# Turning tokens by products with diagonals, and a first gather that alternates with the gate product

## The chip, the core and the metric

The kernel runs on one core of a Trainium2 chip. TensorE (PE) multiplies, VectorE (DVE), ScalarE (ACT) and GpSimd (POOL) work elementwise, and SyncE (SP) issues the DMAs that bring weights from memory. The metric is the time of one execution in microseconds (us), as the median of several; one more execution was taken with a hardware profiler, and all rows below are from that one.

## The reference

A backbone of two layers over 256 latent tokens and, in the first layer, 256 context tokens, with 1024 features. Each layer has a token mixer of four branches and then a mixture of experts (MoE). The change touches the way into the MoE alone:

```python
h = rmsnorm(x, norm2_g) * (1.0 + mod[4]) + mod[3]     # per latent or context token
grp_prob = softmax(h @ w_grp + b_grp)                 # 4 groups, top 1
exp_logits = h @ w_exp + b_exp                        # 8 experts in the group, top 2
# every expert's tokens, gathered in blocks of rows:
hb = silu(xb @ w_gate[e]) * (xb @ w_up[e])
y = hb @ w_down[e]
x = x + mod[5] * (sum over a token's experts of weight * y)
```

There are 32 experts, and each has 6 MB of weights in float32.

## The kernel before

The stream of tokens is kept with features on partitions (`xT`: 128 partitions, 8 blocks of features, n tokens; n is 512 in layer 0 and 256 in layer 1). `moe(l)` does the following in each layer.

The squares of x have been summed in `acc`; `rstd_of` (L475 to L478) sums them over partitions by products with ones, and Ln and Exp on ACT make r, the inverse norm, the same on all partitions. In layer 0 the remaining modulation units (`self.later`, L440, L445, L452) are driven here. `route` scales the router's logits with r (L1267), brings them to tokens on partitions by products with a selection matrix (L1272), adds the bias (L1275) and runs a long chain of small steps on DVE, with a few products between (L1286 to L1417), which ends in `gm`, the masks by which tokens are gathered.

Beside this, the tokens are normed and modulated: L1539 multiplies x with r (blocks alternate between DVE and POOL), L1542 scales and shifts on ACT, L1547 turns 128 x 128 blocks by transposes on PE, and four lines split the turned block into a rounded part and the rest, `hk[0]` and `hk[1]` (L1553 on ACT, then either L1555 on DVE or L1558 on ACT and L1559 on POOL).

`gather` (L1424) multiplies `hk` with the masks, one group of products for each of the 8 blocks of features, and copies each to `xs` (L236 or L238). Two experts share a block of 128 rows. `group` then runs `up` for the gate weights and `up` for the up weights (L1440, 8 steps each), `turned`, `down` (L1482) and `add`.

Weights come in chunks of 1 MB into rings of buffers (`chunk`, L352): an expert has two for gate, two for up, two for down. There are 11 buffers in layer 0 and 15 in layer 1. SP issues the chunks in the program's order, and each issue waits until the buffer that it takes has been read for the last time. A gate product of two experts has two halves: the first reads the first chunk of each expert, the second half their second chunks.

The program's order on each engine is not that of the code: a scheduler places the instructions, so the pieces shown below come from the built programs.

Of the kernel before, what the change touches and what calls it, by code (L numbers as in the profile page):

```python
# [17 lines left out]
P = 128  # L18
D = 1024
# [166 lines left out]
class Net:  # L186
# [1067 lines left out]
            assert not self.main and not self.side and not any(self.left.values())  # L1254


    def route(self, l, n, r):

        nc = self.nc
# [4 lines left out]
        gi, ei, b64 = k[:, 0:4], k[:, 4:12], k[:, 45:53]  # L1264
        baser, capr, first = (self.slots[:, 256 + i * NE:256 + (i + 1) * NE] for i in range(3))
        lt = t([P, n], "lt")
        nc.vector.tensor_tensor(lt, self.lgp[:, 0:n], r, op=ALU.mult)  # L1267
        cum = t([P, nt + 1, NE], "cum", F32R)
        nc.gpsimd.memset(cum[:, 0].bitcast(F32), 0.0)
        p = self.ps("aux")  # L1270
        for i in range(nt):
            nc.tensor.matmul(p[:, i * 64:i * 64 + 36], lt[:, i * P:(i + 1) * P], self.k["sel"], start=True, stop=True)  # L1272
        lg = t([P, nt, 36], "lg")
        nv = n // NL
        nc.vector.tensor_tensor(lg.rearrange("p (v i) e -> p v i e", v=nv),  # L1275
                                p[:, 0:nt * 64].rearrange("p (v i e) -> p v i e", v=nv, e=64)[:, :, :, 0:36],
                                self.brow[:, :, None, :].to_broadcast([P, nv, nt // nv, 36]), op=ALU.add)
        sc = t([P, 8, nt], "sc")
        tt = nc.vector.tensor_tensor

# [123 lines left out]
    def gather(self, l, n, R, sid0, ns):  # L1404

        nc = self.nc
        nt = n // P
        ex = self.ex
        gm = ex.tile([P, nt, 4 * CAP], F32R, tag="gm", name=self.name("gm"), bufs=1)
        iota = self.slots[:, 0:ns]  # L1410
        sm = ex.tile([P, 2, nt], F32, tag="sm", name=self.name("sm"))
        for i in range(2):
            nc.vector.tensor_scalar(sm[:, i], R["s"][i], sid0, None, op0=ALU.subtract)
        for i in range(nt):
            tmp = ex.tile([P, 4 * CAP], F32, tag="gtmp", name=self.name("gtmp"), bufs=EXB[self.l][1])
            nc.vector.tensor_scalar(tmp[:, 0:ns], iota, sm[:, 0, i:i + 1], None, op0=ALU.is_equal)
            nc.vector.scalar_tensor_tensor(gm[:, i, 0:ns], iota, sm[:, 1, i:i + 1], tmp[:, 0:ns], op0=ALU.is_equal,  # L1417
                                           op1=ALU.add)
        xs = ex.tile([P, KD, 4 * CAP], F32, tag="xs", name=self.name("xs"), bufs=EXB[self.l][4])
        for k in range(KD):  # L1420
            p = self.ps("aux")
            for i in range(nt):
                for part, hh in enumerate(self.hk):
                    nc.tensor.matmul(p[:, 0:ns], hh[:, i, k * P:(k + 1) * P], gm[:, i, 0:ns],  # L1424
                                     start=i == 0 and part == 0, stop=i == nt - 1 and part == 1)
            self.copy(xs[:, k, 0:ns], p[:, 0:ns])
        return xs

    def up(self, ws, xs):
# [73 lines left out]
    def moe(self, l):  # L1503
        n = NT if l == 0 else NL
        nt = n // P
        nc, tc = self.nc, self.tc
        gate = self.mod[l][:, 40:48, :]
        a = self.a
        with ExitStack() as st:
            r1, r2 = self.ring1, self.pool(st, f"ring2{l}", RING2[l])  # L1510
            self.rings = [r for i in range(max(RING, RING2[l])) for r in [r1] * (i < RING) + [r2] * (i < RING2[l])]
            self.rt = self.pool(st, f"rt{l}", 1)
            self.slots = self.rt.tile([P, NSLOT], F32, tag="slots", name=f"slots{l}")
            nc.sync.dma_start(self.slots, a["consts"][:, slice(*CO[f"slots{l}"])])
            flat = lambda t: t.rearrange("p k t -> p (k t)")
            half = KD * NT // 2
            if l == 0:
                hk = [flat(self.big16(F32R, "hk")) for i in range(2)]
            else:
                b = flat(self.big16(F32R, "hk"))  # L1520
                hk = [b[:, 0:half], b[:, half:]]
                b = flat(self.big16(F32, "more"))
                more = [b[:, 0:half], b[:, half:], flat(self.xbig)[:, half:]]
                self.rings = [more] * len(more) + self.rings
            self.hk = [h.rearrange("p (i d) -> p i d", d=D) for h in hk]
            with ExitStack() as st2:
                h2p, mw = self.pool(st2, f"h2p{l}", 1), self.pool(st2, f"mw{l}", 4)
                self.work = mw
                r = self.rstd_of(self.acc[::-1], n, D)
                if self.later:  # L1530
                    rings, self.rings = self.rings, [r1]
                    self.drive(self.later)
                    self.rings, self.nchunk, self.later = rings, SHIFT, []
                R = self.route(l, n, r)
                h2 = h2p.tile([P, KD, n], F32, tag="h2", name=f"h2_{l}")
                A, B = self.A2[l], self.mod[l][:, 24:32, :]
                for k in range(KD):
# [5 lines left out]
                for i in range(nt):  # L1543
                    for q in range(2):
                        p = self.ps("mm")
                        for k in range(4):
                            nc.tensor.transpose(p[:, k * P:(k + 1) * P], h2[:, 4 * q + k, i * P:(i + 1) * P], self.ident)  # L1547

                        o = self.hk[0][:, i, q * 512:(q + 1) * 512]
                        lo = self.hk[1][:, i, q * 512:(q + 1) * 512]  # L1550
                        by4 = lambda t: t.rearrange("t (k f) -> t k f", k=4)
                        pv = p.rearrange("t (f k) -> t k f", k=4)
                        nc.scalar.copy(by4(o), pv)  # L1553
                        if q:
                            nc.vector.tensor_tensor(by4(lo), pv, by4(o).bitcast(F32), op=ALU.subtract)  # L1555
                        else:
                            h = self.w2()
                            nc.scalar.copy(by4(h), pv)  # L1558
# [12 lines left out]
            given = 2 * GROUPS[l].count("S")  # L1571
            for i, ranks in enumerate(groups):
                if i % 2 == 0:
                    xs = self.gather(l, n, R, float(i * P), min(2, len(groups) - i) * P)
                ws = [wsrc(r) if r < given else expert(R["tab"][0:1, r:r + 1]) for r in ranks]
                self.group(ws, xs[:, :, i % 2 * P:(i % 2 + 1) * P], R, float(i * P), gate, n, i + 1 == len(groups))
# [8 lines left out]
    def group(self, ws, xs, R, sid0, gate, n, last=False, now=False):  # L1585


        nc = self.nc
# [4 lines left out]
        p = self.up([w[0] for w in ws], xs)  # L1593
# [163 lines left out]
```

## Time and profile before

| | us |
|---|---|
| median of 3 runs | 2396.53 |
| lowest and highest | 2394.87, 2398.5 |
| the profiled execution | 2393.47 |
| its span in the trace | 2391.7 |
| PE busy (share of the span) | 2133.0 (89%) |
| DVE busy | 1240.1 (52%) |
| ACT busy | 767.8 (32%) |
| POOL busy | 471.0 (20%) |

The mean granted clock of PE was 0.967 of full speed. Busy time is an average over stages: in the mixers PE is busy nearly all the time, in the two MoE stages the DMA engines are. A float32 product shows as two records in the trace, so a count of records is twice that of instructions. PEld rows are loads of the stationary operand, PE rows the products; a row of the timeline may join several instructions of one line. What stands in brackets at a row's end is the idle time ahead of it and what ended it.

### The profile page before, as it was taken

The page shows a single profiled execution, that of the slowest core. Times are in us where ns is not written, and L with a number is a line of the kernel's source. Part 1 is how long each engine was busy: PE and PEld are TensorE (multiplying, and loading weights), DVE is VectorE, ACT ScalarE, POOL GpSimd, SP SyncE. Part 2 cuts the span into 40 slices and gives each one's busy share as a digit, 9 for nine tenths or more (in the row PEclk, how much of TensorE's full clock was granted, in tenths as well). Part 3 has the DMA queues.
Part 4 walks back from the last instruction along what each step waited for, and adds up shares of the span by engine and source line. Part 5 has one row for each costly group of instructions (what it writes and reads, how often), then busy time and mean ns, then how long its engine had stood idle before and what let it go on. Part 6 is the DMA issues. An engine that isn't in the chain of part 4 may idle for free. (4 is left out here: it accounts for less than half of the span.)

```text
span 2391.7 us, 30524 instructions
## 1 busy us (share of the span) xinstructions
PE 2133.0 (89%) x11634; PEld 1386.4 (58%) x11634; DVE 1240.1 (52%) x2344; ACT 767.8 (32%) x1394; POOL 471.0 (20%) x469
## 2 busy tenths in 40 slices
PE   6999999999999989989998978988989798877875
PEld 3878777867777753434432368887879642222311
DVE  4398887666434353434423268899777532111211
ACT  3434434356444231000100155555567310000001
POOL 2145443043311020000000033454352100000000
PEclk8999999999999989999999999999999899989998
DMA  8214423423354349999899933333235699999996
GB/s 310 88 56 139 141 100 112 170 77 124 116 183 156 126 197 414 421 407 421 350 421 421 379 124 106 107 110 103 71 108 175 258 382 421 421 421 421 421 421 262
DMA packets 174681, 577.75 MB, mean 242 GB/s; under 512 B 9152, under 2 KB 106048, under 8 KB 121024
## 3 DMA queue, kind: packets, MB, share of 16 engines
q1 hardware_dynamic: 172016, 571.27, 61.4%
q10 hardware_dynamic: 2512, 4.44, 0.5%
q8 instruction: 95, 1.56, 0.3%
q14 instruction: 58, 0.48, 0.1%
HBM read 573.58 MB, written 2.10 MB: 241 GB/s over the span
## 5 line engine op out<-in xcount | busy, mean ns | idle before, releaser
L527 PE MATMUL mm<-hhi,hi 128*128 128x512 f32 (+1 forms) x1216 | 441.4, 364 | 22.7 <-ACT hhi L506 6.8
L1440 PE MATMUL mm<-raw,xs 128*32 128x512 f32 (+2 forms) x1832 | 391.0, 624 | 66.1 <-DMA raw<-in_moe_w_up_dram 44.5
L529 PE MATMUL mm<-hlo,hi 128*128 128x512 f32 (+1 forms) x1216 | 425.0, 350 | 0.6 <-DVE hlo L507 0.6
L530 PE MATMUL mm<-hhi,lo 128*128 128x512 f32 (+1 forms) x1216 | 423.8, 349 | 0.7 <-DVE lo L374 0.7
L374 DVE TENSOR_TENSOR lo<-raw,hi 128x1024 fp32r<-128x1024 f32 x216 | 279.4, 1296 | 160.2 <-ACT hi L371 158.8
L371 ACT CAST hi<-raw 128x1024 fp32r<-128x1024 f32 x216 | 225.1, 1044 | 236.7 <-PE mm L529 163.5
L1440 PEld LDWEIGHTS mm<-raw,xs 128*32 128x32 f32 (+2 forms) x1832 | 106.0, 125 | 308.3 <-issue 178.0
L527 PEld LDWEIGHTS mm<-hhi,hi 128*128 128x128 f32 x1216 | 231.8, 191 | 70.1 <-ACT hhi L506 9.6
L1482 PE MATMUL mm<-raw,hT 128*32 128x512 f32 (+2 forms) x952 | 234.1, 598 | 23.7 <-DMA raw<-in_moe_w_down_dram 13.8
L530 PEld LDWEIGHTS mm<-hhi,lo 128*128 128x128 f32 x1216 | 231.1, 190 | 33.8 <-issue 1.2
L529 PEld LDWEIGHTS mm<-hlo,hi 128*128 128x128 f32 x1216 | 231.7, 191 | 31.6 <-DVE hlo L507 2.1
L1597 DVE TENSOR_TENSOR h<-h,mm 128x512 f32<-128x512 f32 x23 | 15.8, 687 | 369.7 <-PE mm L1440 369.7
L1055 POOL TENSOR_TENSOR acc<-acc,scr 128x512 f32<-128x512 f32 (+1 forms) x4 | 4.0, 995 | 970.8 <-ACT scr L1053 969.9
L882 DVE SCALAR_TENSOR_TENSOR w<-cvpad,vecs,w 128x512 f32<-128x512 f32 (+1 forms) x240 | 161.9, 674 | 3.9
L1482 PEld LDWEIGHTS mm<-raw,hT 128*32 128x32 f32 (+2 forms) x952 | 64.7, 122 | 158.2 <-issue 100.1
L1489 DVE SCALAR_TENSOR_TENSOR yl<-mm,sid,yh 128x512 fp32r<-128x512 f32 x46 | 34.4, 750 | 191.0 <-ACT yh L1488 189.0
L1488 ACT ACTIVATE yh<-mm,sid 128x512 fp32r<-128x512 f32 x46 | 31.6, 688 | 315.9 <-PE mm L1482 315.4
L1035 DVE SCALAR_TENSOR_TENSOR x<-aux,mod,x 128x256 f32<-128x256 f32 x288 | 116.5, 475 | 24.9 <-PE aux L1500 24.4
L1594 ACT ACTIVATE h<-mm 128x512 f32<-128x512 f32 x23 | 13.7, 597 | 277.4 <-PE mm L1440 277.4
L1424 PEld LDWEIGHTS aux<-gm,hk 128*128 128x128 f32 x608 | 79.0, 200 | 28.2 <-issue 20.0
L1424 PE MATMUL aux<-gm,hk 128*128 128x256 f32 (+1 forms) x608 | 86.5, 298 | 7.7 <-DVE gm L1417 7.7
L679 POOL TENSOR_TENSOR w<-w,w 128x256 f32<-128x256 f32 x96 | 89.4, 934 | 18.3 <-DVE w L680 17.8
(337 smaller groups left out, 3575.8 us busy)
## 6 DMA issues: line engine op xcount, KB each, us to landing
raw<-in_moe_w_up_dram SPq DMA_DIRECT2D x119, 1024.0 KB, 17.0
raw<-in_moe_w_down_dram SPq DMA_DIRECT2D x119, 1024.0 KB, 19.7
raw<-in_moe_w_gate_dram SPq DMA_DIRECT2D x110, 1024.0 KB, 19.1
raw<-in_w_in_dram SPq DMA_DIRECT2D x84, 1024.0 KB, 5.0
raw<-in_ada_w_dram SPq DMA_DIRECT2D x48, 1024.0 KB, 5.4
raw<-in_w_branch_dram SPq DMA_DIRECT2D x16, 1024.0 KB, 5.0
more<-in_moe_w_gate_dram SPq DMA_DIRECT2D x12, 1024.0 KB, 19.8
raw<-in_w_out_dram SPq DMA_DIRECT2D x8, 1024.0 KB, 5.0
```

Of the source, the lines that this page charges most:

```text
L371: self.nc.scalar.copy(hi, raw)
L374: eng.tensor_tensor(lo, raw, hi.bitcast(F32), op=ALU.subtract)
L527: nc.tensor.matmul(ps[j], wh, self.hhi[:, kk, 0:n], start=self.first(n, j, kk == 0), stop=False, skip_group_check=True)
L529: nc.tensor.matmul(ps[j], wh, self.hlo[:, kk, 0:n], start=False, stop=False, skip_group_check=True)
L530: nc.tensor.matmul(ps[j], wl, self.hhi[:, kk, 0:n], start=False, stop=kk == 7, skip_group_check=True)
L679: ptt(q4[:, :, B], q4[:, :, B], bc(p4[:, :, A, e:e + 1]), op=ALU.add)
L882: self.nc.vector.scalar_tensor_tensor(dst, s, w(i), dst, op0=ALU.mult, op1=ALU.add)
L1035: nc.vector.scalar_tensor_tensor(x, p[:, s], gate[:, dm, v:v + 1], x, op0=ALU.mult, op1=ALU.add)
L1424: nc.tensor.matmul(p[:, 0:ns], hh[:, i, k * P:(k + 1) * P], gm[:, i, 0:ns], start=i == 0 and part == 0, stop=i == nt - 1 and part == 1)
L1440: nc.tensor.matmul(p[s], xs[:, kk, s], r[:, k, :], start=kk == 0, stop=kk == 7, skip_group_check=True)
L1482: nc.tensor.matmul(p[s], hT[:, 2 * r + k, s], w[:, k, j * 512:(j + 1) * 512], start=r == 0 and k == 0, stop=r == 1 and k == 1, skip_group_ ...
L1489: nc.vector.scalar_tensor_tensor(yl, p, sid[:, 3:4], yh.bitcast(F32), op0=ALU.mult, op1=ALU.subtract)
```

## The change

The turning and the modulation become one product: a block of x (128 features by 128 tokens) is the stationary operand and a diagonal matrix with the modulation's scale (`dg`, 128 x 128) the moving one, so that the result has tokens on partitions. The shift is added by a product of one row with one row: the token's norm (`srow`) times the shift (`rows`). Four such products and one of one row fill a tile of 128 tokens by 512 features, and the eviction multiplies it by r, which is now a column with one number for each token (`rtok`): L1321 on ACT gives the rounded part, L1322 on DVE the rest. There are 8 such tiles in layer 0 and 4 in layer 1. `token_norm` makes `rtok` (L1264) and `srow` (L1271), `token_mod` the diagonals (L1290 on POOL for context tokens, in layer 0 alone; L1292 on ACT) and the shift's rows (8 products L1298). The router's logits are multiplied by r when their bias is added (L1342, once for each 128 tokens). In the first `gather` of a layer, each group of gather products is issued directly ahead of the step of the gate product that needs it.

```diff
+    def token_norm(self, l, n):
+        nt = n // P
+        p = self.ps("aux")
+        for i in range(nt):
+            for j, a in enumerate(self.acc[::-1]):
+                nc.tensor.matmul(p[:, i:i + 1], a[:, i * P:(i + 1) * P], self.ones[:, 0:1], start=i == 0 and j == 0,
+                                 stop=j == 1, skip_group_check=True)
+        r = self.norm.tile([P, 4], F32, tag="rtok", name=f"rtok{l}", bufs=1)[:, 0:nt]
+        nc.scalar.activation(r, p[:, 0:nt], AF.Ln, bias=self.eps, scale=1.0 / D)
+        nc.scalar.activation(r, r, AF.Exp, scale=-0.5)
+        p = self.ps("aux")
+        for j, a in enumerate(self.acc[::-1]):
+            nc.tensor.matmul(p[0:33, 0:n], self.ones[:, 0:33], a, start=j == 0, stop=j == 1)
...
+    def token_mod(self, l, n):
...
+        for v in range(n // NL):
+            nc.gpsimd.tensor_copy(bp[:, :, 32 * v], B[:, :, v])
+            d = self.work.tile([P, KD, P], F32, tag=f"dg{v}", name=f"dg{v}", bufs=1)
+            for k in range(KD):
+                if v:
+                    nc.gpsimd.tensor_scalar(d[:, k], self.ident, self.A2[l][:, k, v:v + 1], None, op0=ALU.mult)
+                else:
+                    nc.scalar.activation(d[:, k], self.ident, AF.Copy, scale=self.A2[l][:, k, v:v + 1])
...
+        for q in range(2):
+            p = self.ps("aux")
+            for k in range(4):
+                nc.tensor.matmul(p[0:33, k * P:(k + 1) * P], bp[:, 4 * q + k, :], self.ident, start=k == 0, stop=k == 3,
+                                 skip_group_check=True)
+            nc.scalar.copy(rows[:, q * 512:(q + 1) * 512], p[0:33])
...
+    def token_rows(self, l, n, r, s, by):
...
+                for k in range(4):
+                    o, x = p[:, k * P:(k + 1) * P], self.xT[:, 4 * q + k, i * P:(i + 1) * P]
+                    nc.tensor.matmul(o, x, by[0][v][:, 4 * q + k], start=k == 0, stop=False, skip_group_check=True)
+                e = slice(32 * v, 32 * v + 1)
+                nc.tensor.matmul(p, s[e, i * P:(i + 1) * P], by[1][e, q * 512:(q + 1) * 512], start=False, stop=True,
+                                 skip_group_check=True)
...
+                nc.scalar.activation(o, pv, AF.Copy, scale=r[:, i:i + 1])
+                nc.vector.scalar_tensor_tensor(lo, pv, r[:, i:i + 1], o.bitcast(F32), op0=ALU.mult, op1=ALU.subtract)
...
-        nc.vector.tensor_tensor(lt, self.lgp[:, 0:n], r, op=ALU.mult)
+        nc.vector.tensor_copy(lt, self.lgp[:, 0:n])
...
+        for i in range(nt):
+            nc.vector.scalar_tensor_tensor(lg[:, i], p[:, i * 64:i * 64 + 36], r[:, i:i + 1], self.brow[:, i * P // NL],
+                                           op0=ALU.mult, op1=ALU.add)
...
+        if first:
+            return xs, rows
+        for k in range(KD):
+            rows(k)
...
+                if rows:
+                    rows(kk)
...
-                h2p, mw = self.pool(st2, f"h2p{l}", 1), self.pool(st2, f"mw{l}", 4)
-                r = self.rstd_of(self.acc[::-1], n, D)
+                self.work = self.pool(st2, f"mw{l}", 2)
+                r, s = self.token_norm(l, n)
...
-                for k in range(KD):
-                    x, o = self.xT[:, k, 0:n], h2[:, k]
-                    (nc.gpsimd if k % 2 else nc.vector).tensor_tensor(o, x, r, op=ALU.mult)
-                    for v in range(n // NL):
-                        c = slice(v * NL, (v + 1) * NL)
-                        nc.scalar.activation(o[:, c], o[:, c], AF.Identity, bias=B[:, k, v:v + 1], scale=A[:, k, v:v + 1])
...
-                            nc.tensor.transpose(p[:, k * P:(k + 1) * P], h2[:, 4 * q + k, i * P:(i + 1) * P], self.ident)
...
-                            nc.gpsimd.tensor_tensor(lo, h, o.bitcast(F32), op=ALU.subtract)
+                self.token_rows(l, n, r, s, by)
```

PE in layer 0, from the norm to the router's small products (L475 the norm's sum, L440 and L452 the late modulation, L1272 the logits turned, L1547 the first transposes), before:

```order
L475 MATMUL aux_6374<-acc_6124,ones 128x512
L440 MATMUL mm_6388<-raw_6382,sT 32x512 x3
L440 MATMUL mm_6388<-raw_6384,sT 32x512 x4
L440 MATMUL mm_6388<-raw_6386,sT 32x512 x4
L452 MATMUL aux_6407<-cst,w_1051_6405 128x4 x4
L1272 MATMUL aux_6417<-cst,lt_6413 128x36 x4
L1547 MATMUL mm_6551<-cst,h_0_6526 128x128 x4
L1547 MATMUL mm_6560<-cst,h_0_6526 128x128
```

and after the change (L1264 and L1271 the norm, L1313 and L1315 the turning, L1298 the shift's rows, L1339 the logits turned):

```order
L1264 MATMUL aux_6371<-ones,acc_6124 128x1
L1271 MATMUL aux_6383<-acc_6124,ones 33x512
L440 MATMUL mm_6397<-raw_6391,sT 32x512 x3
L440 MATMUL mm_6397<-raw_6393,sT 32x512 x4
L440 MATMUL mm_6397<-raw_6395,sT 32x512 x4
L1313 MATMUL mm_6573<-dg_6425,x_6052 128x128 x4
L452 MATMUL aux_6416<-cst,w_1051_6414 128x4 x4
L1298 MATMUL aux_6445<-cst,bp 33x128 x4
L1298 MATMUL aux_6451<-cst,bp 33x128 x4
L1339 MATMUL aux_6461<-cst,lt_6457 128x36 x4
L1315 MATMUL mm_6573<-rows,srow 128x512
```

Seven of the eight L1264 stand just ahead of the second L1271, four products of the first tile have moved ahead of L452, and the eight L1298 stand between L452 and the logits.

DVE in layer 0, at the start of the selection chain (L1539 scales x, L1275 adds the bias, L1286 and the lines behind it are the selection), before:

```order
L1539 TENSOR_TENSOR h_0_6526<-x_6052,w_1045_6377 128x512
L1275 TENSOR_TENSOR lg_6422<-aux_6417,brow_6077 128x144
L1539 TENSOR_TENSOR h_0_6526<-x_6052,w_1045_6377 128x512
L1286 TENSOR_REDUCE sc_6424<-lg_6422 128x4
L1288 TENSOR_TENSOR goh_6426<-lg_6422,sc_6424 128x16
L1298 TENSOR_TENSOR ge_6432<-lg_6422,sc_6424 128x16
L1289 TENSOR_TENSOR goh_6426<-goh_6426,cst 128x16
L1291 TENSOR_REDUCE gohb_6429<-goh_6426 128x4
L1292 TENSOR_TENSOR goh_6426<-goh_6426,gohb_6429 128x16
L1300 TENSOR_REDUCE sc_6424<-ge_6432 128x4
L1303 TENSOR_TENSOR e_0_6437<-lg_6422,goh_6426 128x128
```

and after (L1342 scales and adds the bias, L1352 to L1369 are the same selection steps, L1322 takes the rest of a turned tile):

```order
L1342 SCALAR_TENSOR_TENSOR lg_6466<-aux_6461,rtok_6380,brow_6077 128x36 x4
L1352 TENSOR_REDUCE sc_6471<-lg_6466 128x4
L1354 TENSOR_TENSOR goh_6473<-lg_6466,sc_6471 128x16
L1364 TENSOR_TENSOR ge_6479<-lg_6466,sc_6471 128x16
L1355 TENSOR_TENSOR goh_6473<-goh_6473,cst 128x16
L1357 TENSOR_REDUCE gohb_6476<-goh_6473 128x4
L1322 SCALAR_TENSOR_TENSOR hk_6367<-mm_6573,rtok_6380,hk_6366 128x512
L1358 TENSOR_TENSOR goh_6473<-goh_6473,gohb_6476 128x16
L1366 TENSOR_REDUCE sc_6471<-ge_6479 128x4
L1369 TENSOR_TENSOR e_0_6484<-lg_6466,goh_6473 128x128
L1367 RECIPROCAL sc_6471<-sc_6471 128x4
```

The products with r are gone from DVE, and the first of eight L1322 stands between two steps of the selection; the others follow at similar distances.

PE in layer 1, at the first gather (L1424 or L1491 the gather products, L1440 or L1514 the gate product), before:

```order
L1424 MATMUL aux_15545<-gm_15504,hk_15327 128x256 x4
L1424 MATMUL aux_15551<-gm_15504,hk_15327 128x256 x4
L1424 MATMUL aux_15557<-gm_15504,hk_15327 128x256 x4
L1440 MATMUL mm_15564<-raw_15565,xs_15514 64x512
L1440 MATMUL mm_15564<-raw_15567,xs_15514 64x512
```

and after:

```order
L1491 MATMUL aux_15555<-gm_15538,hk_15348 128x256 x4
L1491 MATMUL aux_15563<-gm_15538,hk_15348 128x256 x3
L1514 MATMUL mm_15550<-raw_15551,xs_15548 64x512
L1514 MATMUL mm_15550<-raw_15553,xs_15548 64x512
L1491 MATMUL aux_15563<-gm_15538,hk_15348 128x256
L1491 MATMUL aux_15571<-gm_15538,hk_15348 128x256 x4
L1514 MATMUL mm_15550<-raw_15551,xs_15548 64x512
L1514 MATMUL mm_15550<-raw_15553,xs_15548 64x512
L1514 MATMUL mm_15550<-raw_15551,xs_15548 64x512
L1514 MATMUL mm_15550<-raw_15553,xs_15548 64x512
```

The gate product no longer waits for the last gather group: its first step has two groups of the gather ahead of it, and the rest alternates.

## Rows read from the trace of the kernel before

**Rows 1.** The page, moved GB/s in 40 equal slices of the span.

```profile
GB/s 310 88 56 139 141 100 112 170 77 124 116 183 156 126 197 414 421 407 421 350 421 421 379 124 106 107 110 103 71 108 175 258 382 421 421 421 421 421 421 262
```

**Rows 2.** 20-us windows inside the plateaus: busy time by engine, PEclk, DMA share, GB/s.

```profile
920.00:940.00 20.00, 16.69 (x109) 5.97 (x102) 10.60 (x29) 0.60 (x1) 0.00 (x0) 0.97 1.02 422
...
2020.00:2040.00 20.00, 11.55 (x68) 2.50 (x64) 0.00 (x0) 0.60 (x1) 0.00 (x0) 0.95 1.01 421
```

**Rows 3.** Windows of 1 us at the edges of the two holes.

```profile
884.00:885.00 1.00, 1.00 (x6) 1.00 (x6) 0.84 (x6) 0.00 (x0) 0.00 (x0) 0.50 0.19 74
897.00:898.00 1.00, 1.00 (x8) 0.41 (x6) 0.00 (x0) 0.00 (x0) 0.00 (x0) 1.00 0.39 57
1919.00:1920.00 1.00, 1.00 (x10) 0.87 (x10) 0.51 (x2) 0.42 (x2) 0.00 (x0) 1.00 0.58 238
1924.00:1925.00 1.00, 1.00 (x6) 0.29 (x4) 0.00 (x0) 0.00 (x0) 0.00 (x0) 1.00 0.62 82
```

**Rows 4.** Timeline, SP's DMA issues: start, duration, line, tile, count.

```profile
860.70 35.95 SPq L352 DMA_DIRECT2D raw<-in_moe_w_down_dram  x4
...
1923.49 0.33 SPq L352 DMA_DIRECT2D raw<-in_moe_w_gate_dram  x1
```

**Rows 5.** Timeline, layer 0 from the norm to the gate product.

```profile
854.60 1.13 PE L475 MATMUL aux<-acc,ones 128*128 128x512 f32 x2
...
859.69 1.05 PE L452 MATMUL aux<-cst,w 128*128 128x4 f32 x8 [1.25 <-ACT w L445]
...
864.03 0.16 DVE L1286 TENSOR_REDUCE sc<-lg 128x4 f32<-128x16 f32 x1
...
877.32 1.36 DVE L1366 TENSOR_TENSOR tmp<-O,slot 128x128 f32<-128x128 f32 x1
...
882.25 2.11 PE L1424 MATMUL aux<-gm,hk 128*128 128x256 f32 x7 [4.20 <-DVE gm L1417]
...
892.64 13.95 PE L1440 MATMUL mm<-raw,xs 128*64 128x512 f32 x64
```

**Rows 6.** Prices: timeline rows, groups of the page's part 5, a window of L1424 alone.

```profile
907.97 1.95 PE L1398 MATMUL aux<-cst,s 128*128 128x128 f32 x16
...
L1489 DVE SCALAR_TENSOR_TENSOR yl<-mm,sid,yh 128x512 fp32r<-128x512 f32 x46 | 34.4, 750 | 191.0 <-ACT yh L1488 189.0
L1488 ACT ACTIVATE yh<-mm,sid 128x512 fp32r<-128x512 f32 x46 | 31.6, 688 | 315.9 <-PE mm L1482 315.4
...
891.80 0.42 DVE L236 COPY xs<-aux 128x256 f32<-128x256 f32 x1 [1.47 <-PE aux L1424]
...
888.00:892.00 4.00, 4.00 (x36) 4.00 (x35) 1.00 0.00 0
```

**Rows 7.** Timeline, layer 1 from the norm to the gate product.

```profile
1894.54 0.70 PE L475 MATMUL aux<-acc,ones 128*128 128x256 f32 x2 [0.26 <-DVE acc L1055]
...
1898.94 0.15 DVE L1286 TENSOR_REDUCE sc<-lg 128x2 f32<-128x8 f32 x1
...
1904.07 1.26 DVE L1325 TENSOR_TENSOR cum<-cum,Os 128x32 fp32r<-128x32 f32 x1
...
1913.56 2.75 PE L1424 MATMUL aux<-gm,hk 128*128 128x256 f32 x11 [3.49 <-DVE gm L1417]
...
1919.81 12.67 PE L1440 MATMUL mm<-raw,xs 128*64 128x512 f32 x58
```

**Rows 8.** 5-us windows with the granted clock (PEclk, after the busy times).

```profile
860.00:865.00 5.00, 2.02 (x18) 1.80 (x17) 4.87 (x12) 2.59 (x7) 3.56 (x3) 0.89 1.01 423
865.00:870.00 5.00, 3.12 (x10) 1.92 (x10) 4.64 (x30) 4.85 (x11) 0.70 (x2) 0.50 1.01 426
880.00:885.00 5.00, 2.75 (x11) 2.58 (x12) 4.84 (x22) 0.00 (x0) 0.02 (x1) 0.59 0.84 349
1910.00:1915.00 5.00, 1.51 (x7) 1.44 (x7) 4.64 (x30) 0.18 (x1) 0.00 (x0) 0.50 1.01 419
1915.00:1920.00 5.00, 5.00 (x30) 4.87 (x30) 1.63 (x5) 1.20 (x4) 0.00 (x0) 0.64 0.94 385
```

More of the change, by code (lines that the diff above doesn't have):

```diff
@@ L1254, in mixer @@
             assert not self.main and not self.side and not any(self.left.values())
+    def token_norm(self, l, n):
+        nc = self.nc
+        nt = n // P
[10 more added lines that the diff above has]
+            nc.tensor.matmul(p[0:33, 0:n], self.ones[:, 0:33], a, start=j == 0, stop=j == 1)
+        s = self.work.tile([33, n], F32, tag="srow", name="srow", bufs=1)
+        nc.scalar.activation(s, p[0:33, 0:n], AF.Ln, bias=self.eps[0:33], scale=1.0 / D)
+        nc.scalar.activation(s, s, AF.Exp, scale=0.5)
+        return r, s
@@ new lines, in token_mod @@
+    def token_mod(self, l, n):
+        nc = self.nc
+        B = self.mod[l][:, 24:32, :]
+        bp = self.work.tile([P, KD, 33], F32, tag="bp", name="bp", bufs=1)
+        nc.gpsimd.memset(bp, 0.0)
+        dg = []
+        for v in range(n // NL):
[6 more added lines that the diff above has]
+                    nc.scalar.activation(d[:, k], self.ident, AF.Copy, scale=self.A2[l][:, k, v:v + 1])
+            dg.append(d)
+        rows = self.work.tile([33, D], F32, tag="rows", name="rows", bufs=1)
+        for q in range(2):
[4 more added lines that the diff above has]
+            nc.scalar.copy(rows[:, q * 512:(q + 1) * 512], p[0:33])
+        return dg, rows
@@ new lines, in token_rows @@
+    def token_rows(self, l, n, r, s, by):
+        nc = self.nc
+        by4 = lambda t: t.rearrange("t (k f) -> t k f", k=4)
+        for q in range(2):
+            for i in range(n // P):
+                v = i * P // NL
+                p = self.ps("mm")
+                for k in range(4):
[4 more added lines that the diff above has]
+                                 skip_group_check=True)
+                o = by4(self.hk[0][:, i, q * 512:(q + 1) * 512])
+                lo = by4(self.hk[1][:, i, q * 512:(q + 1) * 512])
+                pv = p.rearrange("t (f k) -> t k f", k=4)
+                nc.scalar.activation(o, pv, AF.Copy, scale=r[:, i:i + 1])
+                nc.vector.scalar_tensor_tensor(lo, pv, r[:, i:i + 1], o.bitcast(F32), op0=ALU.mult, op1=ALU.subtract)
@@ L1273, in route @@
         lg = t([P, nt, 36], "lg")
[L1274 to L1277, printed above, removed]
+        for i in range(nt):
+            nc.vector.scalar_tensor_tensor(lg[:, i], p[:, i * 64:i * 64 + 36], r[:, i:i + 1], self.brow[:, i * P // NL],
+                                           op0=ALU.mult, op1=ALU.add)
         sc = t([P, 8, nt], "sc")
@@ L1402, in spread, with gather @@
                 nc.scalar.copy(R[src, i], p[:, 0:n])
-    def gather(self, l, n, R, sid0, ns):
+    def gather(self, l, n, R, sid0, ns, first=False):
         nc = self.nc
@@ L1419, in gather, with rows @@
         xs = ex.tile([P, KD, 4 * CAP], F32, tag="xs", name=self.name("xs"), bufs=EXB[self.l][4])
-        for k in range(KD):
+        def rows(k):
             p = self.ps("aux")
@@ L1426, in gather, with up @@
             self.copy(xs[:, k, 0:ns], p[:, 0:ns])
+        if first:
+            return xs, rows
+        for k in range(KD):
+            rows(k)
         return xs
-    def up(self, ws, xs):
+    def up(self, ws, xs, rows=None):
         nc = self.nc
@@ L1526, in moe @@
             with ExitStack() as st2:
-                h2p, mw = self.pool(st2, f"h2p{l}", 1), self.pool(st2, f"mw{l}", 4)
-                self.work = mw
-                r = self.rstd_of(self.acc[::-1], n, D)
+                self.work = self.pool(st2, f"mw{l}", 2)
+                r, s = self.token_norm(l, n)
                 if self.later:
@@ L1533, in moe @@
                     self.rings, self.nchunk, self.later = rings, SHIFT, []
+                by = self.token_mod(l, n)
                 R = self.route(l, n, r)
-                h2 = h2p.tile([P, KD, n], F32, tag="h2", name=f"h2_{l}")
-                A, B = self.A2[l], self.mod[l][:, 24:32, :]
-                for k in range(KD):
-                    x, o = self.xT[:, k, 0:n], h2[:, k]
-                    (nc.gpsimd if k % 2 else nc.vector).tensor_tensor(o, x, r, op=ALU.mult)
-                    for v in range(n // NL):
-                        c = slice(v * NL, (v + 1) * NL)
-                        nc.scalar.activation(o[:, c], o[:, c], AF.Identity, bias=B[:, k, v:v + 1], scale=A[:, k, v:v + 1])
[L1543 to L1546, printed above, removed]
-                            nc.tensor.transpose(p[:, k * P:(k + 1) * P], h2[:, 4 * q + k, i * P:(i + 1) * P], self.ident)
[L1549 to L1558, printed above, removed]
-                            nc.gpsimd.tensor_tensor(lo, h, o.bitcast(F32), op=ALU.subtract)
+                self.token_rows(l, n, r, s, by)
             self.ex = self.pool(st, f"ex{l}", 2)
@@ L1572, in moe @@
             for i, ranks in enumerate(groups):
-                if i % 2 == 0:
+                rows = None
+                if i == 0:
+                    xs, rows = self.gather(l, n, R, 0.0, 2 * P, True)
+                elif i % 2 == 0:
                     xs = self.gather(l, n, R, float(i * P), min(2, len(groups) - i) * P)
                 ws = [wsrc(r) if r < given else expert(R["tab"][0:1, r:r + 1]) for r in ranks]
-                self.group(ws, xs[:, :, i % 2 * P:(i % 2 + 1) * P], R, float(i * P), gate, n, i + 1 == len(groups))
+                self.group(ws, xs[:, :, i % 2 * P:(i % 2 + 1) * P], R, float(i * P), gate, n, i + 1 == len(groups), rows=rows)
             if l + 1 < DEPTH:
@@ L1583, in moe, with group @@
             self.rings = [self.ring1]
-    def group(self, ws, xs, R, sid0, gate, n, last=False, now=False):
+    def group(self, ws, xs, R, sid0, gate, n, last=False, now=False, rows=None):
         nc = self.nc
@@ L1592, in group @@
         o = h.rearrange("s (r k f) -> s r k f", r=2, k=2)
-        p = self.up([w[0] for w in ws], xs)
+        p = self.up([w[0] for w in ws], xs, rows)
         nc.scalar.activation(o, src(p), AF.Silu)
```

## The prediction

> **What bounds the kernel.** I read the page's forty slices first. In the GB/s row [rows 1] two plateaus of 421 GB/s stand out: one from slice 16 to 23, the experts of layer 0, one from slice 33 to the end, the experts of layer 1. Inside them the DMA engines are full and PE is not: 16.69 of 20 us busy with a DMA share of 1.02 in layer 0, 11.55 of 20 with 1.01 in layer 1 [rows 2]. So in both plateaus the end is set by when the stream of weight chunks starts and by nothing that PE, DVE or ACT do later. A chunk is 1 MB, at 421 GB/s 2.5 us.
>
> The stream does not start cleanly. Before each plateau the ring of weight buffers is full and nobody frees one. The one-microsecond windows show the edges: in layer 0 the DMA share falls to 0.19 at 884 us and comes back only at 897 (a hole of 13 us); in layer 1 it falls at 1919 and comes back at 1924, a hole of 4.9 us from 1919.6 to 1924.4 by those windows' shares [rows 3]. SP, which issues all chunks in order, shows the same thing: a stretch that starts at 860.70 lasts 35.95 us since its last DMA has to wait for a buffer, and in layer 1 the next issue comes at 1923.49 [rows 4]. What frees the buffer is the first gate product (L1440), and that starts at the end of the gather: 892.64 in layer 0 [rows 5], 1919.81 in layer 1 [rows 7]. A whole gate product is 32 records of 0.215 us (6.9 us). Its first half frees two chunks, 3.4 us after its start (896.1 and 1923.25, where SP's issues follow), its second half two more. Hence the only thing that the change can move for the whole kernel is the pair of moments "first two chunks free" and "gate product done", once in each layer. The most that layer 1 can gain is its hole, 4.9 us; layer 0 has 13.
>
> **Layer 0, up to the selection.** Between the second L475 at 854.60 and the router's small products PE now has seven products L1264 more (a weight load each, so the price of L452, 1.05 us for 8 records, two records an instruction: 0.26) = 1.8 us; L1271 costs what the L475 that it replaces did. The four L1313 that the order puts in front of L452 take 4 x 0.244 (L1398: 16 records, 8 instructions, 1.95 us [rows 6]) = 1.0 us and lie in the 1.25 us that PE waits there for ACT [rows 5]. Eight L1298 add 8 x 0.244 = 1.95, on the path. L1339 then starts near 864.3 and no longer waits for r on 512 columns, but four scaled additions (0.2 each) follow where one stood. The first reduction of the selection, 864.03 before, comes near 866.0: +2.0 us.
>
> **Layer 0, the selection.** From that reduction to the gather the trace has 882.25 - 864.03 = 18.2 us. About 4.7 us of it is work of the old turning in the way: L1555 subtractions on DVE (some 1.6 visible), DVE operations stretched while POOL's L1559 ran (L1366 took 1.36 us, where its like take 0.3, and one L1348 likewise: 2.0), ACT and PE steps queued behind evictions and transposes (1.1). POOL's part and the transposes go. In their place eight L1322 of 0.75 (by L1489, which has the same form) stand in DVE's order; two fall in waits that DVE has anyway, six are visible: 4.5 us, and 0.5 for the interleaved products. Net +0.3. The gather starts near 884.5, and its last mask (1.65 us later) is there at 886.2.
>
> **Layer 0, first gather with the gate product between.** After the last mask, at full clock: 59 gather products of 0.118 (36 records, two of them in part, fill 4 us [rows 6]; 7.0), eight steps of the gate product of 0.86 (6.9), and 1.2 for steps that wait for the copy of xs (0.42 each [rows 6], mostly beside the next gather group) = 15.1. The product is done at 901.3 (before 899.5), but its first half already at 893.9 (before 896.1), since only half of the gather stands ahead of it. So two chunks flow 2.2 us earlier, and then the stream pauses: the third needs the whole product, 901.3 + 1.1 (SP's issue to first data, as before) = 902.4. Before, the third followed the first two without a pause at 902.2. Sum for layer 0: **+0.2 us**. If the products run at the lower clock for long, +2 instead.
>
> **Layer 1.** Here token_mod has half the diagonals and no late modulation is waited for: 0.73 + 0.5 + 1.95 us from 1894.54 bring L1339 to 1897.7 and the first reduction to 1898.8 (before 1898.94). The chain to the gather was 1913.56 - 1898.94 = 14.6 us [rows 7]. What goes is a hold by L1539 (0.7), DVE stretched beside POOL (L1325 took 1.26 where 0.2 is its like, and L1346 likewise: 2.0) and one visible L1555 (0.5): 3.2. What comes is two visible L1322, 1.5. The gather starts near 1911.75 (-1.8). Up to the first two free chunks there are 20 gather products and 4 steps: 2.4 + 3.4 = 5.8 at full clock. The granted clock was 0.50 when the old gather began and came back inside it [rows 8]; with the same 4.7 us of half clock as before, 2.4 more, and 0.5 of waits: 1920.45, first data 1921.5 (before 1924.4). The whole product is done at 1925.8, the third chunk follows at 1926.9 where it was 1929.4. Sum for layer 1: **-2.4 us**.
>
> Together -2.2: 2393.47 becomes 2391.3 for the profiled execution. The median of the runs shown is 3.06 above the profiled one, so **2394.3**.
>
> **Costs that the trace of before does not show.** The one-row products L1315 (128x512 from one partition): between the 0.244 of L1313 and the 1.13 that an L475 took with its tail [rows 5]; I take 0.9, near the second, since the moving columns are the same (at 0.244 the tiles of layer 0 would end 5 us earlier, with the chain then held by L1322 alone, no more than 0.5 us off the sum). L1321 (eviction with a scale) and L1322: L1488 and L1489 at 0.69 and 0.75, against 0.6 and 0.67 of what they replace. The 16 diagonals (8 on ACT, 8 on POOL, layer 0) lie beside L440 and the norm; were they late, up to 2.5 us. Bounds for layer 0: -2.5 (no L1322 visible) to +8 (rival C); for layer 1: -4.9 (its hole) to +1.5 (all L1322 visible and no gain from POOL).
>
> **Rival B: the clock stays up.** The rows show the granted clock at 0.89 from 860, 0.50 from 865 and 0.59 from 880, and 0.50 at 1910 [rows 8], each time after several microseconds in which PE had only small products between waits. In the changed kernel PE is busy without a gap from 855 to 880 and from 1894 to 1905. If the level of 2.4 GHz holds through the gathers, layer 1's first chunks are free 2.9 us before the forecast, inside the old plateau, and the hole of 4.9 us is gone; layer 0 gains about 1 (0.8 on the products inside the selection). -5.9: **2390.6**. Against it: between the last turning product and the gather there are still some 5 us of selection, as there were before the old falls. The Trainium skill ("TensorE: Matmul & The Clock Gate", Part 1) calls the reduced clock the default that activity lifts; the rows agree as far as the fall after sparse work goes, and no row here has such a dense stretch just ahead of a gather.
>
> **Rival C: slower.** DVE's order is fixed, and the first L1322 stands before the selection's sixth step. Each L1322 waits for a tile of PE (four L1313 and one L1315) and for ACT's L1321. At full clock a tile is 1.9 us and the chain is hardly held. At 0.50, the level that the trace has over just these microseconds [rows 8], a tile is 2 x (0.96 + 0.86) = 3.6, eight tiles from 864.7 end at 893.8, and the selection's steps, the rank products behind the tiles on PE too, follow their pace: gather at about 892 instead of 884.5, +7.5 in layer 0; in layer 1 four tiles end at 1912.3, the gather at 1913.5, +1 after the lost gain. **2405**. It decides once the tiles take over 2.5 us each.
>
> **Rival D: the alternation costs.** If each of the eight steps waits for its own copy with nothing between (0.6 us each, 4.8 a layer), the product ends 3.6 later in each layer: layer 0 +3.8, layer 1 +1.2: **2401**. Against it: the order has a gather group or two ahead of each step.
>
> **How the numbers follow.** Forecast 0.53, B 0.21, C 0.15, D 0.11. Two runs of this kernel differ by up to 0.15%, so 0.2% (4.8 us) is the least that counts: faster is below 2391.7, slower above 2401.3. The forecast's own range is 2391 to 2398. Faster: B's larger part (0.19) and the low end of the forecast (0.08) = 0.27. Slower: C (0.15) and a third of D (0.04), less a little of C that lands short = 0.17. The rest, 0.56, is within. For 8 in 10 the range takes in B down to 2388.5 and D up to 2401.5.
>
> **What would show it.** Right: the holes' ends in the DMA windows at about 895 and 1921.5 with a second, short hole near 901 in layer 0; the first L1440 step right after the first gather group; gather starts near 884.5 and 1911.75; L1322 at 0.75 without long waits ahead. A granted clock of 1.0 at 1912 speaks for B, a clock of 0.5 at 866 and idle DVE ahead of L1322 for C, PE waits of 0.5 us before each step of the gate product for D. I am wrong if the plateaus do not move with the first release, or if the mixers' stretch before 854 changes, where nothing was touched.

## The result, and the profile after

The changed kernel takes 2415.9 us (median of 4, 2410.47 to 2417.37) against 2395.8 for the kernel before: a ratio of 1.0081, 95% interval 1.0067 to 1.0096. It is slower by 20 us, where I forecast 2 us less. The profiled execution has a span of 2415.6 us, 23.9 more than the one before.

The timeline shows where. These are SP's rows of the changed kernel; L1588 loads the slot table and marks the start of a MoE stage, the second column is the length of a row:

```profile
858.26 0.43 SPq L1588 DMA_DIRECT2D slots<-in_consts_dram  x1
...
864.28 50.20 SPq L352 DMA_DIRECT2D raw<-in_moe_w_down_dram  x4
915.29 23.44 SPq L352 DMA_DIRECT2D raw<-in_moe_w_gate_dram  x8
...
1914.28 0.33 SPq L1588 DMA_DIRECT2D slots<-in_consts_dram  x1
...
1945.97 0.33 SPq L352 DMA_DIRECT2D raw<-in_moe_w_gate_dram  x1
```

SP's long wait in layer 0 is 50.20 us where it was 35.95 [rows 4]. I measure each stage from its own slot table, since the mixers ahead of it, in which the change moved no instruction, differ from one execution to the next: in the eleven profiled executions of this study the first table is loaded between 854.8 and 859.0. From that mark, layer 0's gather starts at 43.71 (before 27.15) and layer 1's at 22.15 (before 20.79). The 23.9 us are, from SP's rows: 3.2 ahead of layer 0; 19.9 from its table to the second set of up chunks (80.71 against 60.79), 16.6 of them before the gather starts; -1.6 from there to layer 1's table; and 2.4 from that table to the end (501.32 against 498.93).

The DVE rows of the selection, with one of ACT between, say what the gather waited for. In brackets stand the idle time ahead of a row and what ended it:

```profile
876.46 0.75 DVE L1322 SCALAR_TENSOR_TENSOR hk<-mm,rtok,hk 128x512 fp32r<-128x512 f32 x1 [2.19 <-ACT hk L1321]
...
879.74 0.69 ACT L1321 ACTIVATE hk<-mm,rtok 128x512 fp32r<-128x512 f32 x1 [2.13 <-PE mm L1315]
...
899.71 0.75 DVE L1322 SCALAR_TENSOR_TENSOR hk<-mm,rtok,hk 128x512 fp32r<-128x512 f32 x1 [3.00 <-ACT hk L1321]
```

Seven of the eight L1322 wait for ACT, 12.7 us in all (two are shown), and ACT's L1321 waits for PE. PE's rows in the same stretch, one tile after another:

```profile
867.85 1.12 PE L1315 MATMUL mm<-rows,srow 1*128 1x512 f32 x2
868.90 1.16 PE L1313 MATMUL mm<-dg,x 128*128 128x128 f32 x8
869.99 1.70 PE L1315 MATMUL mm<-rows,srow 1*128 1x512 f32 x2
871.62 2.08 PE L1313 MATMUL mm<-dg,x 128*128 128x128 f32 x8
873.63 2.07 PE L1315 MATMUL mm<-rows,srow 1*128 1x512 f32 x2
875.63 2.08 PE L1313 MATMUL mm<-dg,x 128*128 128x128 f32 x8
...
896.88 2.07 PE L1315 MATMUL mm<-rows,srow 1*128 1x512 f32 x2
...
901.97 3.15 PE L1491 MATMUL aux<-gm,hk 128*128 128x256 f32 x12 [3.02 <-DVE gm L1483]
```

The same two lines take 1.1 us each at first and 2.1 from 871 on: a tile goes from 2 us to 4. The last ends at 898.95, and the gather follows 3.0 us later. The windows give the reason (busy time of PE, PEld, DVE, ACT and POOL, then the granted clock, the DMA share and GB/s):

```profile
865.00:870.00 5.00, 5.00 (x36) 3.88 (x35) 1.91 (x11) 1.95 (x4) 0.00 (x0) 1.00 1.01 423
870.00:875.00 5.00, 5.00 (x13) 2.56 (x12) 3.39 (x15) 0.69 (x1) 0.29 (x1) 0.54 1.02 421
875.00:880.00 5.00, 5.00 (x12) 2.65 (x12) 1.88 (x10) 1.15 (x3) 0.29 (x1) 0.50 1.01 421
885.00:890.00 5.00, 5.00 (x15) 2.98 (x13) 2.20 (x12) 0.95 (x2) 0.00 (x0) 0.50 0.48 200
...
900.00:905.00 5.00, 3.03 (x12) 2.71 (x12) 4.81 (x23) 0.00 (x0) 0.00 (x0) 0.50 0.00 0
905.00:910.00 5.00, 4.93 (x19) 2.26 (x19) 0.15 (x3) 0.37 (x1) 0.00 (x0) 0.71 0.00 0
```

PE is busy in all of 865 to 890, and yet the granted clock falls from 1.00 to 0.50 (of the levels 2.4 and 1.2 GHz, the lower) and stays there to 907, when the gate product has begun. Before, the clock fell too [rows 8], but PE then had only short pieces of work; here it has no gap.

### The profile page after: what moved, and what is told of

Same layout as the page of the kernel before. It is cut to its first block, busy times and chain, and to the rows that moved or that the text cites. A ratio compares the mean times of both kernels' runs of the same rounds, so it can differ in the third digit from the quotient of the medians.

```text
span 2415.6 us, 30778 instructions
## 1 busy us (share of the span) xinstructions
PE 2178.0 (90%) x11762; PEld 1412.5 (58%) x11762; DVE 1235.8 (51%) x2346; ACT 762.8 (32%) x1388; POOL 458.2 (19%) x468
## 5 line engine op out<-in xcount | busy, mean ns | idle before, releaser
L1514 PE MATMUL mm<-raw,xs 128*32 128x512 f32 (+2 forms) x1832 | 395.8, 630 | 67.0 <-DMA raw<-in_moe_w_up_dram 46.2
L1514 PEld LDWEIGHTS mm<-raw,xs 128*32 128x32 f32 (+2 forms) x1832 | 108.5, 126 | 303.1 <-issue 170.0
L1491 PEld LDWEIGHTS aux<-gm,hk 128*128 128x128 f32 x608 | 77.5, 195 | 39.2 <-issue 39.2
L1491 PE MATMUL aux<-gm,hk 128*128 128x256 f32 (+1 forms) x608 | 87.5, 295 | 6.9 <-DVE gm L1483 6.9
L679 POOL TENSOR_TENSOR w<-w,w 128x256 f32<-128x256 f32 x96 | 89.4, 934 | 18.3 <-DVE w L680 18.2
```

The costliest lines, as they stand in the source:

```text
L679: ptt(q4[:, :, B], q4[:, :, B], bc(p4[:, :, A, e:e + 1]), op=ALU.add)
```

## The experiments

Two questions were open: how much of the 20 us is the turning and how much the alternation, and why the clock falls while PE is busy. Of each kernel one execution was profiled, and what is told of clocks and rows is from that one. This table gives every run, with the start of the first gather and the first issue after the long wait (in layer 0) counted from the stage's slot table, and the time from layer 1's table to the span's end:

| kernel | median, us | ratio to before (95%) | gather 0 | issue 0 | gather 1 | layer 1 to end |
|---|---|---|---|---|---|---|
| before | 2394.1 to 2395.8 | | 27.15 | 42.35 | 20.79 | 498.93 |
| changed | 2415.9 | 1.0081 (1.0067 to 1.0096) | 43.71 | 57.03 | 22.15 | 501.32 |
| 1 alternation only | 2400.2 | 1.0018 (1.0009 to 1.0026) | 27.12 | 40.17 | 20.81 | 499.70 |
| 2 turning only | 2412.1 | 1.0077 (1.0061 to 1.0092) | 42.98 | 57.54 | 19.21 | 496.44 |
| 3 no row product | 2398.9 | 1.0013 (1.0002 to 1.0024) | 28.80 | 41.61 | 20.12 | 499.17 |
| 4 wide row product | 2398.2 | 1.0020 (1.0009 to 1.0031) | 28.49 | 40.75 | 19.86 | 499.44 |
| 5 wide, no alternation | 2395.0 | 1.0005 (0.9996 to 1.0013) | 28.49 | 42.76 | 20.03 | 498.49 |
| 6 rest on POOL | 2414.4 | 1.0089 (1.0074 to 1.0103) | 41.77 | 56.72 | 22.75 | 500.02 |
| 7 row product on 33 | 2402.8 | 1.0041 (1.0027 to 1.0056) | 30.64 | 46.11 | 21.09 | 498.61 |
| 8 early selection | 2395.0 | 1.0002 (0.9993 to 1.0011) | 30.05 | 44.13 | 17.86 | 495.19 |
| 9 new in layer 1 only | 2395.5 | 1.0000 (0.9990 to 1.0010) | 27.14 | 42.57 | 17.86 | 495.28 |

**1. The alternation alone**, put into the kernel before:

```diff
+                if rows:
+                    rows(kk)
                 for i, r in enumerate(raw):
```

> The turning of before, with the first gather alternating with the gate product. Theory 1 (the one-row products: each adds as many columns as the four products of its tile, so that at half clock a tile takes 4 us, and the selection, in order behind L1322 on DVE and behind the tiles on PE, follows the tiles): the alternation is a side matter, worth -3 to +4 us, 2393 to 2400. Theory 2 (the alternation is what costs: two chunks come early, then the stream pauses until the slower gate product is done): most of the 20 us is here, 2405 to 2415.

It costs 4 us, at the edge of what theory 1 allowed and far from theory 2. PE's rows show the price, at a granted clock of 1.00. Each step of four records takes 1.01 us to the next row, nine gather records 1.27 and seven 1.09:

```profile
889.34 1.08 PE L1448 MATMUL mm<-raw,xs 128*64 128x512 f32 x4
890.35 1.34 PE L1425 MATMUL aux<-gm,hk 128*128 128x256 f32 x9
891.62 1.08 PE L1448 MATMUL mm<-raw,xs 128*64 128x512 f32 x4
892.62 1.09 PE L1425 MATMUL aux<-gm,hk 128*128 128x256 f32 x7
```

In one piece, as in experiment 5, 64 records of the gate and the up product take 13.95 us (0.87 for four). The 64 gather records take 9.53 there, with the clock at 0.50 at 888 and 889; at the full clock eight of them take about 0.94 (estimated from the 36 that fill 4 us in [rows 6]):

```profile
887.11 9.53 PE L1494 MATMUL aux<-gm,hk 128*128 128x256 f32 x64 [3.02 <-DVE gm L1486]
896.57 13.95 PE L1517 MATMUL mm<-raw,xs 128*64 128x512 f32 x64
```

The first chunks do come 2.2 us earlier in experiment 1 (40.17), and then the stream stops, since the slower gate product has not freed the next buffers:

```profile
900.00:901.00 1.00, 1.00 (x8) 0.42 (x6) 0.30 (x1) 0.00 (x0) 0.00 (x0) 1.00 1.03 434
901.00:902.00 1.00, 1.00 (x8) 0.50 (x5) 0.00 (x0) 0.00 (x0) 0.00 (x0) 1.00 0.45 188
902.00:903.00 1.00, 1.00 (x5) 0.48 (x7) 0.97 (x3) 0.37 (x1) 0.00 (x0) 1.00 0.00 0
```

The second set of up chunks starts 63.89 us after the table instead of 60.79, so the early start ends as a loss of 3.1 us in layer 0, and the time from layer 1's table to the end is 0.8 longer.

**2. The turning alone.**

```diff
-                if i == 0:
-                    xs, rows = self.gather(l, n, R, 0.0, 2 * P, True)
-                elif i % 2 == 0:
+                if i % 2 == 0:
```

> The changed kernel without the alternation. Theory 1: layer 0's gather starts some 15 us later than before against the start of the stage, 2409 to 2418. Theory 2: 2393 to 2400.

As theory 1 says. The second set of up chunks is 15.2 us late in layer 0. In layer 1, where there are four tiles, the clock stayed at 1.00 up to the last of them, and the stage is 2.5 us shorter than before. Four tiles do not lose the clock in every execution: in experiment 6 it fell in layer 1 too (0.81 from 1920, 0.50 from 1925), as in the changed kernel.

**3. No row product.**

```diff
-                nc.tensor.matmul(p, s[e, i * P:(i + 1) * P], by[1][e, q * 512:(q + 1) * 512], start=False, stop=True,
-                                 skip_group_check=True)
```

> The changed kernel without the one-row products L1315 (the shift of the modulation is left out of the turned tokens; everything that prepares it stays). Theory 1: a tile takes 1.0 to 2.1 us, L1322 hardly waits, the gather of layer 0 starts 12 to 16 us earlier than in the changed kernel, 2394 to 2402. Theory 2: no more than 5 us back, 2410 or more.

Layer 0's gather starts 14.9 us earlier than in the changed kernel. So the eight one-row products carry the loss, but this does not yet say whether by their columns or by the clock.

**4. The row product on 128 partitions.** The norm's row and the shift's rows stand in tiles that are zero elsewhere; PE gets as many products and columns as in the changed kernel, in the same order.

```diff
-                nc.tensor.matmul(p, s[e, i * P:(i + 1) * P], by[1][e, q * 512:(q + 1) * 512], start=False, stop=True,
+                nc.tensor.matmul(p, s[:, i * P:(i + 1) * P], by[1][:, q * 512:(q + 1) * 512], start=False, stop=True,
```

> The changed kernel with the shift's product on 128 partitions (the norm's row and the shift's rows padded with zeros), as many columns as before. Theory 1a (the half clock comes from products that use a single row of the array): the granted clock is back at 1.0 within the first four tiles, a tile takes 2 us, the gather of layer 0 starts 8 to 12 us earlier, 2400 to 2408. Theory 1b (the number of rows does not matter, the clock falls for what came before and these products don't lift it): the granted clock stays at 0.50 to the gather, 2412 to 2418.

Theory 1a, and by more than it asked. Its windows over the tiles, to be held against those of the changed kernel above:

```profile
865.00:870.00 5.00, 5.00 (x36) 4.13 (x36) 1.99 (x11) 1.95 (x4) 0.00 (x0) 1.00 1.01 423
870.00:875.00 5.00, 5.00 (x31) 3.75 (x30) 4.79 (x24) 2.11 (x4) 0.29 (x1) 1.00 1.00 418
875.00:880.00 5.00, 4.89 (x25) 3.24 (x23) 4.52 (x23) 1.68 (x4) 0.30 (x1) 1.00 1.01 421
```

and PE's rows:

```profile
868.73 1.05 PE L1317 MATMUL mm<-dg,x 128*128 128x128 f32 x8
869.62 1.02 PE L1318 MATMUL mm<-rows,srow 128*128 128x512 f32 x2
870.48 1.05 PE L1317 MATMUL mm<-dg,x 128*128 128x128 f32 x8
```

The clock never falls over the tiles, a tile takes 1.75 us from start to start, and 17.7 us come back by the medians (2415.9 to 2398.2). Up to 867.8 the two kernels' PE rows agree within 0.1 us, so what came before the tiles is not the cause. One thing is mixed with the clock: before it falls, the changed kernel's first tile takes 2.14 us (867.85 to 869.99), so at 1.00 too the one-row tile is the slower one; experiment 7 parts the two. The Trainium skill ("TensorE: Matmul & The Clock Gate", Part 1) has a busy PE release the lower clock; here busy time alone did not, and the measurement decides: 5.00 of 5.00 us busy at a granted 0.50.

**5. The wide row product without the alternation.**

> The shift's product on 128 partitions and no alternation. Theory 1a (one-row products keep the granted clock at its lower level, and the alternation costs 3 to 5 us a layer): the gather of layer 0 starts 28 us after the load of the slot table (before 27), runs at the full clock from its start and ends by 38; layer 1 gains 2.5 to 4.9; 2389 to 2394. Rival (the wide product's gain in the last run came with the alternation, and the turning by products costs some us in any form): 2396 to 2402.

2395.0 against 2394.1, no difference that can be told from none, and just above the first theory's range. Layer 0 meets that theory's numbers (28.49, and the gather ends at 37.95), but not its full clock: that was 0.50 at 888 and 889. Layer 1 gains only 0.4 of the 2.5 that it asked. Its gather starts 0.8 earlier than before, and then takes 6.79 us (before 6.32, in experiment 2 5.52), with the clock at 0.50 from 1915 to 1920. The loss of the changed kernel is thereby split: the one-row products, with the clock under them, and the alternation. What remains of the new turning shows in no median.

**6. The rest of a tile on ACT and POOL.** From experiment 2:

```diff
-                nc.vector.scalar_tensor_tensor(lo, pv, r[:, i:i + 1], o.bitcast(F32), op0=ALU.mult, op1=ALU.subtract)
+                h = self.w2()
+                nc.scalar.activation(by4(h), pv, AF.Copy, scale=r[:, i:i + 1])
+                nc.gpsimd.tensor_tensor(self.hk[1][:, i, q * 512:(q + 1) * 512], h, self.hk[0][:, i, q * 512:(q + 1) * 512].bitcast(F32), op=ALU.subtract)
```

> The changed kernel without the alternation, one-row products kept, but the rest of each turned tile is made by ACT (a scaled copy) and POOL (a subtraction), so that nothing of the turning stands on DVE. Theory A (the tiles' pace on PE sets the end: eight tiles of 4 us, and the gather needs all of them): the gather of layer 0 still starts 42 to 46 us after the load of the slot table, 2408 to 2415. Theory B (the selection is held because L1322 stands in DVE's order): the gather starts at 30 to 36, 2396 to 2404.

Theory A: with nothing of the turning left on DVE the gather starts at 41.77 instead of 42.98. On PE it stands behind all eight tiles:

```profile
891.92 2.07 PE L1315 MATMUL mm<-rows,srow 1*128 1x512 f32 x2
897.21 10.21 PE L1493 MATMUL aux<-gm,hk 128*128 128x256 f32 x64 [3.22 <-DVE gm L1485]
```

The last tile ends at 894.0. DVE had the tokens' places in the blocks (L1435) by 886.0, and the mask for which the gather then waits 3.22 us was itself held by POOL's part of the last tile (L1324). So the waits ahead of L1322 are a symptom: eight tiles of 4 us set the time, and no more than 3.2 us are left for anything else.

**7. The row product on 33 partitions**, two of them with data:

> As the wide product without the alternation, but on 33 partitions (0 and 32 carry the two kinds of tokens, the rest zeros). If each product with few rows holds the clock down, as the one-row product does: granted clock 0.50 from 870 on, 2408 to 2413. If it is only the single row: as the product on 128 partitions, 2389 to 2394.

For the clock this is not settled. In the profiled execution (2395.0) it was 1.00 over the tiles, but the other three took 2400.65 to 2405.6 and were not profiled. The profile shows something else:

```profile
865.00 1.12 PE L1318 MATMUL mm<-rows,srow 33*128 33x512 f32 x2
866.05 1.16 PE L1317 MATMUL mm<-dg,x 128*128 128x128 f32 x8
867.14 1.12 PE L1318 MATMUL mm<-rows,srow 33*128 33x512 f32 x2
```

A tile takes 2.14 us at a clock of 1.00, as the changed kernel's first did, where experiment 4 has 1.75. From the first shift product to the last tile's end, with the same products between, it is 18.0 us here, 16.0 in experiment 4 and 31.1 in the changed kernel. So of the 15.1 us that the padding to 128 partitions takes off this stretch, some 2 are there without a fallen clock, and 13 go with the clock (an estimate, with 33 partitions standing for one at the full clock). The second set of up chunks starts 3.4 us later than in experiment 5 (64.55 against 61.20).

**8. The selection ahead of the late modulation.** From experiment 5, `route` is called first and makes the diagonals and the shift's rows right behind L1339's products:

```diff
-                R = self.route(l, n, r)
+                R, by = self.route(l, n, r, lambda: self.token_mod(l, n))
```

> As the wide product without the alternation, but the selection is issued ahead of the late modulation and of the shift's rows: L1339's products stand right behind the norm's on PE. Theory 1 (the gather waits for the selection's end as much as for the tiles): layer 0's gather starts 25 to 27 us after the load of the slot table instead of 28.5, its masks are ready with it, and layer 1's gather 2 us earlier; 2387 to 2392. Rival (PE's queue of eight tiles sets the start of the gather, and they end no earlier): 2393 to 2396, as without this step.

By its numbers the rival, in layer 0: the gather starts at 30.05, later than in experiment 5, since PE's tiles end no earlier (28.0 after the table, 25.5 in experiment 5). But the clock has a part in this that neither theory had:

```profile
860.00:865.00 5.00, 5.00 (x26) 3.63 (x26) 2.47 (x13) 4.56 (x13) 0.89 (x1) 0.71 0.96 380
875.00:880.00 5.00, 5.00 (x19) 3.49 (x19) 3.21 (x14) 0.87 (x2) 0.00 (x0) 0.66 1.00 419
```

It fell twice while PE was busy, the second time over the third and fourth tile, with the padded product in them; it was back at 1.00 before the last four. By the rows of experiment 5 this cost some 3.3 us (an estimate: 1.6 in L1302, which took 3.56 us for 1.94, and 1.7 in the two tiles), more than the 2.5 by which the tiles end later. So the theory was not tried at the full clock, and padding alone does not keep the clock up in every order. Layer 1's stage is 3.7 us shorter than before. The median is the same.

**9. The new way in layer 1 alone**, with experiment 8's order, the old turning in layer 0.

> Layer 0 turned as before the change, layer 1 by products with diagonals: the shift's product on 128 partitions, no alternation, the selection issued early. Theory 1 (the products pay in layer 1, where the last run's stage from the slot table's load to the end was 3.7 us shorter, and cost up to 2 in layer 0): 2390 to 2393, faster than both by its interval. Rival (the stage's length varies by that much by itself): 2394 to 2397.

Layer 1's stage was 3.65 us shorter in the profile, as in experiment 8, and layer 0's as before; the median did not move (2395.46 against 2394.6). In this profile the stretch from layer 0's second set of up chunks to layer 1's table (the rest of layer 0's experts and the mixers of layer 1) was 7 us longer than in that of before, with the same order of instructions on PE. The other profiles give 973.5 to 980.2 us for it (before 976.9), this one 984.3. The 7 us come in many steps of about 1 us, most of them after 1500. Whether that is chance, or something takes the gain back, stays open. No version here beats the kernel before.

## Why the prediction was wrong

- **What bounds the kernel** was right, with both moments that I named. The first two chunks come 14.7 us later in layer 0, but the plateau, by the second set of up chunks, 19.9 later: it follows the end of the gate product. In experiment 1 the first release is 2.2 earlier and the plateau 3.1 later, so "move with the first release", as I put the sign, was too simple. The loss of layer 0 arrived at the end.
- **Up to the selection** was right: the first reduction comes 1.6 us later against the table (10.55 for 8.93); I had 2.0.
- **The selection** is the step that failed. I wrote "Net +0.3" and the gather at 2.3 us later, on the ground that the products run at the full clock. The stretch took 33.2 us where I had 18.5 (before 18.2). At the full clock the working itself was good: in experiment 5, with the padded product, the stretch takes 17.95 and a tile 1.75 where I had 1.9; the one-row tile itself takes 2.14 as long as the clock is up, and L1322 its 0.75.
- The argument under it, that PE "busy without a gap" speaks for the higher clock (rival B's ground too), is wrong for this kernel: with products of one row between, PE was busy by the profile and the clock fell. Experiment 4 shows that these products make the difference, with the order and the columns unchanged. What rule the clock follows stays open: it held over four such tiles in layer 1 of experiment 2, and fell with padded ones in experiment 8.
- **Rival C** named the place, the mechanism and the point from which it decides (tiles of over 2.5 us), and got 0.15. Its price was too low as well: 4.0 us a tile instead of 3.6, the gather 16.6 later than before instead of 10 (at 892 it stood ahead of the end of its own tiles, 893.8), and 2405 for 2415.9. Its path by DVE's order was not the one that mattered (experiment 6).
- **The alternation** was mis-sized. From the first gather product to the end of the gate product I had 16.8 us with it (884.5 to 901.3); experiment 4 has 19.1, experiment 1 19.9. Without it, experiment 5 has 16.4. The cost is not the wait for xs that I charged with 1.2 us, since PE shows no idle time there, but records that take longer when the two kinds alternate. That the early chunks would be followed by a pause was foreseen. Rival D, at 0.11, was nearer in price (2401 for the 2400.2 of experiment 1), but by luck: its waits of 0.6 us are not there.
- **Layer 1**: the -2.4 was forecast with the alternation. Experiment 2 comes near it without (-2.5), where the clock stayed up over the four tiles, so that the agreement is in part luck. In the changed kernel the clock fell at about 1925, in the third tile, and the stage lost 2.4 instead.

## What to carry to other kernels

A product with one row costs as many columns as one with 128, and in a run of them the clock can fall, which here doubled the time of the products and of all that PE did around them: read the granted clock beside the busy time, and try padding such a product to all partitions when the operand can be made with zeros. It kept the clock up in experiments 4 and 5, and made a tile 0.4 us shorter besides; experiment 8 shows that it is no guarantee. When a stream waits for a buffer, ask when the last of the needed buffers is free, not the first: an early first chunk bought by a later second one is a loss. Where a forecast hangs on the clock, give both levels a case of their own size, since here the level alone was worth some 13 us in layer 0's tiles.

## What was not expected of the hardware

Rows of zeros were enough: at least 126 of the 128 rows of experiment 4's product are zero, and the granted clock stayed at 1.00 over all eight tiles, against 0.50 from 871 to 907 in the changed kernel. A product on few partitions lengthens a tile at the full clock, too: 2.14 us with 1 or 33 partitions, 1.75 with 128, for the same columns; why was not tried. The records of two kinds of products take longer in alternation (1.01 us for four instead of 0.87), though PE shows no idle time between them; which part of PE's work that is was not tried. And a stretch that no edit touches varies: from the second set of up chunks to layer 1's table it lasted 973.5 to 984.3 us in these executions, more than most of the effects asked after here, which is why the stages were read from their own marks.
